# A hybrid attention and delta-rule block on one core: the inverse roots of the delta rule's norms, given out turn by turn

## The chip, the cores and the metric

The kernel runs on one core of one Trainium2 chip. The metric is the device time of one execution in microseconds; the median of three runs of the kernel before is 1054.85 us (1052.07 to 1058.07). TensorE (PE in the profile) does the matrix products and transposes, VectorE (DVE), ScalarE (ACT) and GpSimd (POOL) the rest, and SyncE (SP) issues most transfers. Each engine works through its own queue in order.

## The reference

One layer of a streaming encoder on 512 frames of width 1024, with 16 meta tokens ahead. After a layer norm, one projection `h @ w_in` feeds two mixers. One is attention with 8 heads of 64 and a forget gate ("fox" in the names of the kernel). The other is a gated delta rule ("gdn") with 8 heads of 128: queries, keys and values go through a causal convolution of four taps and a silu, then

```python
q_c = _l2norm(q_c); k_c = _l2norm(k_c)          # x * rsqrt(sum(x*x) + 1e-6)
# in chunks of 64: k, v, beta, decay -> triangular solve, state update, o
o = o * rsqrt(mean(square(o)) + 1e-6) * gdn_norm_w
o = o * silu(z_b)
mixed = sigmoid(gate_a) * (y_a @ w_out_a) + sigmoid(gate_b) * (y_b @ w_out_b)
h = _layer_norm(ALPHA * h + mixed @ w_o)
h = _layer_norm(ALPHA * h + (silu(h @ w_gate) * (h @ w_up)) @ w_down)
```

The two `rsqrt` that the change concerns are those of the norms of q and k, and that of the output `o`, one of each for every delta-rule head.

## The kernel before

The core runs through three stretches: the input (norm and transposes) and the mixers until some 570 us of the span, then the output projections, then the feed-forward network. All products are made in parts of a split of the fp32 operands (`x_hi`, `x_lo` by `wh_`, `wl_`).

**The mixer** is a loop over units (L1240), each a projection of 128 columns of `w_in`: `q`, `k`, `v` and `z` of the eight delta-rule heads, and `qa`, `ka`, `va` of the four pairs of attention heads. TensorE's products of a unit are the main stream. After every few of them `tick` (L627) lets side tasks put in their own instructions. A side task is a Python generator that yields `at(time, banks, uses)`: the planner's estimate of when it may go on, the accumulator banks it needs, and the engines that must not be too far behind. The planner keeps an estimated clock for each engine (`est_t`), works out with costs of its own when an operand is ready (`rdy`), and from that the order of the instructions on TensorE, VectorE, ScalarE and GpSimd is fixed when the kernel is built. What stands between two yields goes out in one piece. `SELF` is the planner's delay between two dependent operations of one engine (0.13 us), `MARGIN` a reserve of 1 us on an estimated arrival. At run time each engine takes its instructions in that order and waits where an operand is not there.

**The side tasks of a delta-rule head.** `conv_finish` (L648) takes a unit's accumulator `ps_q`, `ps_k` or `ps_v` and adds the taps: the first on ScalarE, three on VectorE (tiles `c_q`, `c_k`, `c_v`); after the third the accumulator is free. A unit cannot begin before the one two earlier is free. `gdn_prepare` (L713) sums the squares of q and k (`ss`), scales k into `kn`, takes the nine inverse roots for each row (`rsqrt`, L217; tiles `rst_kq` and `rsy_kq`), makes from them `rq` and `bk`, and then the products `psgm` and `psg` of k with k and with q, which VectorE scales into `nm` and `ea`. `rsqrt` is an initial guess from the bits (two operations) and three Newton turns of three operations, eleven in all, each dependent on the one before.

**The side tasks of a group of two heads.** There are four groups, 0 to 3. `gdn_invert` (L797) runs 31 steps of two dependent VectorE operations (`tmp`, `t`) on the 32x32 blocks of both heads, with a yield after every operation. The result goes out to memory (`td`) and comes back in another layout (`tm`, `pm`, `pmm`); then TensorE joins the blocks (`w_g`, `l_g`). `gdn_chunk` runs the state through four chunks. `gdn_finish` (L935) takes the root of the output's mean square (`ov`, then `rst_o` and `rsy_o` of four values a row), GpSimd scales `o` by it (L948), TensorE transposes it (`oT`), and VectorE multiplies it into `y_b`.

**Attention.** The task behind a `qa` unit copies its accumulator into `q_stack` on VectorE and ScalarE, which frees it.

**GpSimd's queue** also issues the transfers `wl_*` (the low parts of the weights, added in flight), and masks (`ea`). SyncE's queue issues weight loads and the round trip of the inversion.

Of the kernel before, what the change touches and what calls it, by code (L numbers as in the profile page):

```python
# [8 lines left out]
F32 = mybir.dt.float32  # L9
F32R = mybir.dt.float32r  # L10
BF16 = mybir.dt.bfloat16
I32 = mybir.dt.int32
AF = mybir.ActivationFunctionType
ALU = mybir.AluOpType
# [4 lines left out]
P = 128  # L19
# [21 lines left out]
LOOK, MARGIN, CAP = 0.4, 1.0, 0.6  # L41
BUSY = {'dve': 3.0, 'act': 1.0}
LAT, SELF, DMA_LAT, DMA_FINE = 0.15, 0.13, 2.3, 2.5
# [34 lines left out]
def hybrid_block(ctx, tc, x, meta_tokens, ln_in_g, ln_in_b, w_in, b_f, conv_w, a_log, dt_bias,  # L78
# [10 lines left out]
    small = ctx.enter_context(tc.tile_pool(name="small", bufs=4))  # L89
# [6 lines left out]
    est_t = dict.fromkeys(("pe", "act", "dve", "pool", "sp"), 0.0)  # L96
# [3 lines left out]
    def tname(v):  # L100
        t = getattr(v, "tensor", None)
        return getattr(t, "name", None)

    def after(when, name, eng, same=0.0):
        t, by = when.get(name, (0.0, eng))
        return t + (same if by == eng else LAT)
# [20 lines left out]
    def xbank(name):  # L127
        i = min((i for i in order if i not in held),
                key=lambda i: max(after(wrote, banks.get(i, ""), ""), after(read, banks.get(i, ""), "")) if held_on[0] else 0.0)
        order.remove(i)  # L130
        order.append(i)
        t = recycle(("x", i), 1, ps_x.tile([P, 512], F32, tag=f"x{i}", name=name, bufs=1))
        banks[i] = tname(t)
        if held_on[0]:
            held.add(i)
        return t
# [3 lines left out]
    def done(*tiles):  # L140
        for t in tiles:
            held.difference_update([i for i in range(4) if banks.get(i) == tname(t)])
# [56 lines left out]
    class Ordered:  # L199
# [3 lines left out]
        def __getattr__(self, op):  # L203
            fn = getattr(self.eng, op)

            def call(*a, **k):
                ins = fn(*a, **k)  # L207
                account(self.name, op, a, k)
                if pinned[0] and self.name in PINS and op != "dma_start":
# [4 lines left out]
    pe, act, dve, pool, sp = (Ordered(e, n) for e, n in ((nc.tensor, "pe"), (nc.scalar, "act"), (nc.vector, "dve"),  # L214
                                                         (nc.gpsimd, "pool"), (nc.sync, "sp")))

    def rsqrt(v, n, name, eng=nc.vector):  # L217
        rows = v.shape[0]
        y = small.tile([P, n], F32, tag=f"rs_y{n}", name=f"rsy_{name}")[:rows]
        t = small.tile([P, n], F32, tag=f"rs_t{n}", name=f"rst_{name}")[:rows]  # L220
        dve.tensor_scalar(t.bitcast(I32), v.bitcast(I32), 1, None, ALU.logical_shift_right)
        dve.tensor_scalar(y.bitcast(I32), t.bitcast(I32), -1, 0x5F3759DF, ALU.mult, ALU.add)
        for _ in range(3):
            eng.tensor_mul(t, y, y)
            if eng is pool:
                eng.tensor_mul(t, t, v)
                eng.tensor_scalar(t, t, -0.5, 1.5, ALU.mult, ALU.add)
                eng.tensor_mul(y, y, t)
            else:
                eng.scalar_tensor_tensor(t, t, -0.5, v, ALU.mult, ALU.mult)  # L230
                eng.scalar_tensor_tensor(y, t, 1.5, y, ALU.add, ALU.mult)
        return y

    class Pinned:
        def __init__(self, eng):
# [225 lines left out]
    def scaled0(i, eng):  # L461
        gi, k = divmod(i, KT)
        c0 = PAD if gi == 0 else PAD + META + 2 * P
        n = META + 2 * P if gi == 0 else 2 * P
        hf = p1.tile([P, META + 2 * P], F32, tag="hf", name=f"hf{gi}_{k}", bufs=HF)[:, :n]
        g, b = prm[:, k:k + 1], prm[:, 8 + k:9 + k]
        if eng is act_:
            eng.activation(hf, hfs[i][:, :n], AF.Identity, bias=b, scale=g)
        else:
            eng.tensor_scalar(hf, hfs[i][:, :n], g, b, ALU.mult, ALU.add)  # L470
        hfs[i] = hf, x_hi[:, k, c0:c0 + n], x_lo[:, k, c0:c0 + n]
# [4 lines left out]
    def low0(i, eng):  # L476
        eng.tensor_sub(hfs[i][2], hfs[i][0], hfs[i][1].bitcast(F32))
# [13 lines left out]
    for step, *a in START:  # L491
        dict(E=lambda: act_.activation(warm, warm, AF.Exp), F=gate_load, b=lambda t, j: sum_half(t, j), m=meta_sums, v=meta_var, i=invert, y=polish, n=norm, M=meta_norm, p=prm_first,
             W=lambda n: split_high(n), w=lambda n, e: split_low(n, engines[e]), T=transposed,
             f=lambda i, e: scaled0(i, engines[e]), h=high0, l=lambda i, e: low0(i, engines[e]),
# [99 lines left out]
    RS = pool if ON_POOL else dve  # L594
    side = []

    def rdy(*aps):
        return max(after(wrote, tname(v), "") for v in aps) + MARGIN

    def at(t, banks=0, uses=""):  # L600
        return t, banks, uses
# [111 lines left out]
    def gdn_prepare(hd, st):  # L713
        h, hh = hd["h"], hd["hh"]
# [4 lines left out]
        ss = small.tile([P, 9], F32, tag="ss", name=f"ss{h}")  # L719
# [24 lines left out]
        dve.tensor_tensor(kn[:, 0:4, :], by_chunk(psk), kd[:, 0:4].unsqueeze(2).broadcast_to([P, 4, P]), ALU.mult)  # L744
        dve.tensor_scalar(kn[:META, 4, :], psm[:META, :P], kd[:META, 4:5], None, ALU.mult)
        done(psk, psm)
        rs = rsqrt(ss, 9, f"kq{h}", RS)
        rq = hd["rq"] = small.tile([P, 4], F32, tag="rq", name=f"rq{h}", bufs=5)
        RS.tensor_scalar(rq, rs[:, 4:8], P ** -0.5, None, ALU.mult)
        RS.tensor_mul(rs, rs, ss)  # L750
# [184 lines left out]
    def gdn_finish(hd, st):  # L935
        h, o, rq = hd["h"], hd["o"], hd["rq"]
        ov = small.tile([P, 4], F32, tag="ov", name=f"ov{h}")
        yield at(rdy(o), 0, "act")
        scr = gp.tile([P, P], F32, tag="scr", name=f"oscr{h}", bufs=1)
        for c in range(NT):  # L940
            act.activation(scr, o[:, c, :], AF.Square, accum_out=ov[:, c:c + 1])
        yield at(rdy(ov))
        RS.tensor_mul(ov, ov, rq)
        RS.tensor_mul(ov, ov, rq)
        RS.tensor_scalar(ov, ov, 1.0 / P, NORM_EPS, ALU.mult, ALU.add)
        ro = rsqrt(ov, 4, f"o{h}", RS)
        RS.tensor_mul(ro, ro, rq)
        pool.tensor_tensor(o, o, ro.unsqueeze(2).broadcast_to([P, NT, P]), ALU.mult)  # L948
        yield at(rdy(o), 1)
        pt = xbank(f"oT{h}")  # L950
        for c in range(NT):
            pe.transpose(pt[:, c * P:(c + 1) * P], o[:, c, :], ident)
        dve.scalar_tensor_tensor(y_b[h], pt, gdn_w, y_b[h], ALU.mult, ALU.mult)
        done(pt)
        if h < 4:
            sp.dma_start(y_d[h // 2, :, h % 2], y_b[h])
        st["finished"] += 1
# [205 lines left out]
    for g in range(4):  # L1163
        for step in ORDERS[min(g, len(ORDERS) - 1)].split():
            h = 2 * g + int(step[1])
            if step[0] in "qkv":
                w = "qkv".index(step[0])
                unit(f"{step[0]}{h}", (C_QB, C_KB, C_VB)[w] + h * P, conv_halves,
                     lambda ps, h=h, w=w: conv_finish(h, w, ps))
# [70 lines left out]
    for u, d in enumerate(units):  # L1240
# [24 lines left out]
        for n, (o, c) in enumerate(passes):  # L1265
# [6 lines left out]
            if d["name"] == "f":  # L1272
                o, low = [v[:6 * HEADS] for v in o], None
# [414 lines left out]
    for j, u in enumerate(units_f):  # L1688
# [19 lines left out]
        p1, t, v = (fin.tile([P, 256], F32, tag="u2", name=f"u{i}_{j}", bufs=5) for i in range(3))  # L1708
# [77 lines left out]
    ov = out.rearrange("(t p) d -> p t d", p=P)  # L1786
# [88 lines left out]
```

## Time and profile before

| | |
|---|---|
| median of three runs | 1054.85 us |
| the profiled execution | 1061.21 us, span 1059.5 us |
| mean granted clock of TensorE | 0.976 of full speed |
| busy, share of the span | PE 94%, DVE 65%, ACT 48%, POOL 31% |
| chain that ended last, by engine | PE 55%, DVE 21%, issue 7%, DMA 6%, ACT 5%, POOL 2% |

The profile is of one execution, which took 0.6% more than the median. Busy time of an engine is the time in which it has an instruction in work. The chain goes back from the last instruction to what released each step. "Granted clock" is the share of TensorE's full clock that it was given. An arrow `x<-y` in a wait says who waited for whom; in an operation it is output and input. Names have their buffer numbers left out, so `c_v` is that of any head.

### The profile page before, as it was taken

The numbers are of one execution on the slowest core, as the hardware profiler recorded it, in microseconds if no ns is written. First come the engines' busy times: TensorE is split into PE (matmuls) and PEld (weight loads), VectorE is DVE, ScalarE is ACT, GpSimd is POOL, SyncE is SP. The second block draws the span as 40 slices with busy tenths as digits, with TensorE's granted clock in tenths as the row PEclk, the third lists the DMA queues.
The fourth block names the chain that finished last, engine by engine and source line by source line (L and its number), as shares of the span: only waits on it lengthen the run. The fifth ranks groups of instructions, "written<-read, shape, count | busy, mean of one in ns | idle before, by whom it ended". The sixth has DMA issues, their size and how long they took to land.

```text
span 1059.5 us, 17755 instructions
## 1 busy us (share of the span) xinstructions
PE 996.5 (94%) x6765; PEld 890.1 (84%) x6765; DVE 683.8 (65%) x1487; ACT 513.0 (48%) x1039; POOL 327.2 (31%) x338
## 2 busy tenths in 40 slices
PE   5998999999999999999999999988999999999995
PEld 4887998779888898877887888788999999988885
DVE  7446586367936884582153655787998998962436
ACT  6466566554664567454563224744435344531121
POOL 5223212202230122211026200555555556226005
PEclk9998999998999999999999999998999999999998
DMA  7587645626763485467677335525332442344322
GB/s 220 133 182 165 135 107 127 149 51 158 153 142 83 101 196 126 83 150 164 163 194 180 114 110 175 104 61 137 88 115 81 119 120 80 100 140 125 94 80 79
DMA packets 171585, 134.70 MB, mean 127 GB/s; under 512 B 19820, under 2 KB 151180, under 8 KB 171500
## 3 DMA queue, kind: packets, MB, share of 16 engines
q1 hardware_dynamic: 161788, 98.39, 32.9%
q0 software_dynamic: 9712, 35.18, 17.6%
q8 instruction: 53, 0.87, 0.3%
q14 instruction: 32, 0.26, 0.1%
HBM read 90.90 MB, written 8.57 MB: 94 GB/s over the span
## 4 chain that ended last, share of the span: by engine, by line
PE 55%; DVE 21%; issue 7%; DMA 6%; ACT 5%; POOL 2%; SPq 0%; DVEq 0%; POOLq 0%; ACTq 0%
PE d L1366 3%; PE d L1364 3%; PE d L1365 3%; PE ps_v L207 3%; PE px L1454 3%; PE ptm L207 3%; PE o L240 3%; PE ps_q L207 2%; PE ps_ga L207 2%; PE ps_z L207 2%; PE ps_gb L207 2%; PE ps_va L207 2%; PE ps_k L207 2%; PE po L1321 2%; PE po L1319 2%
## 5 line engine op out<-in xcount | busy, mean ns | idle before, releaser
L285 DVE TENSOR_TENSOR wl_d<-wr_d,wh_d 128x1024 fp32r<-128x1024 f32 x18 | 22.7, 1263 | 51.4 <-ACT wh_d L283 51.4
L283 ACT CAST wh_d<-wr_d 128x1024 fp32r<-128x1024 f32 x18 | 18.9, 1050 | 65.9 <-PE d L1366 44.0
L1488 POOL TENSOR_TENSOR wr_a<-wr_a,sums 128x512 f32<-128x512 f32 x22 | 29.1, 1323 | 57.1 <-DVE wl_a L1428 56.9
L207 DVE TENSOR_TENSOR tmp<-n,t 34x31 f32<-34x31 f32 (+15 forms) x124 | 42.8, 345 | 2.0
L207 DVE TENSOR_TENSOR t<-t,tmp 34x31 f32<-34x31 f32 (+15 forms) x124 | 42.4, 342 | 1.9
L1365 PE MATMUL d<-wl_d,f_h 128*128 128x512 f32 (+1 forms) x104 | 39.7, 381 | 0.0
L1364 PE MATMUL d<-wh_d,f_h 128*128 128x512 f32 (+1 forms) x104 | 39.6, 381 | 0.0
L1454 PE MATMUL pa<-v_h,wh_a 128*128 128x256 f32 x160 | 39.3, 279 | 0.0
L1454 PE MATMUL pa<-v_h,wl_a 128*128 128x256 f32 x160 | 39.1, 280 | 0.0
L283 ACT CAST wh_wo<-wr_wo 128x512 fp32r<-128x512 f32 (+1 forms) x16 | 13.3, 836 | 40.5 <-PE po L1320 13.8
L285 DVE TENSOR_TENSOR wl_wo<-wr_wo,wh_wo 128x512 fp32r<-128x512 f32 (+1 forms) x16 | 22.5, 1418 | 15.2 <-ACT wh_wo L283 15.2
L1428 DVE TENSOR_TENSOR wlo_b<-wr_b,whi_b 128x1024 fp32r<-128x1024 f32 x11 | 21.7, 1976 | 16.4 <-ACT whi_b L1427 16.4
L1454 PE MATMUL px<-v_h,rb 128*128 128x256 f32 x176 | 26.5, 295 | 4.5 <-DMA rb<-sums 4.5
L1454 PEld LDWEIGHTS pa<-v_h,wh_a 128*128 128x128 f32 x160 | 30.2, 189 | 0.0
L1673 ACT ACTIVATE res<-res 128x512 f32<-128x512 f32 x11 | 7.0, 633 | 47.7 <-DVE res L1738 47.7
L1454 PEld LDWEIGHTS pa<-v_h,wl_a 128*128 128x128 f32 x160 | 30.0, 187 | 0.0
L207 ACT COPY o<-ks 128x128 f32<-128x128 f32 x32 | 8.5, 266 | 44.2 <-DVE r L207 44.2
L207 DVE SCALAR_TENSOR_TENSOR r<-ks,nbeg,bv 128x128 f32<-128x128 f32 x32 | 11.2, 351 | 28.6 <-PE ks L207 23.5
L1454 PEld LDWEIGHTS px<-v_h,rb 128*128 128x128 f32 x176 | 24.2, 203 | 4.7 <-DMA rb<-sums 4.7
L1427 ACT CAST whi_b<-spare_raw 128x1024 fp32r<-128x1024 f32 x10 | 10.5, 1052 | 35.4 <-PE pd L1454 35.4
L207 PE MATMUL ps_z<-x_hi,wh_z 128*128 128x512 f32 x64 | 27.4, 427 | 0.0
L207 PE MATMUL ps_z<-x_lo,wh_z 128*128 128x512 f32 x64 | 27.2, 425 | 0.0
(800 smaller groups left out, 3681.6 us busy)
## 6 DMA issues: line engine op xcount, KB each, us to landing
wr_d<-in_w_down_dram SPq DMA_DIRECT2D x18, 512.0 KB, 3.7
spare_raw<-in_w_gate_dram SPq DMA_DIRECT2D x11, 512.0 KB
wr_b<-in_w_up_dram SPq DMA_DIRECT2D x11, 512.0 KB, 3.8
wr_a<-in_w_gate_dram SPq DMA_DIRECT2D x11, 512.0 KB
wr_a<-in_w_up_dram SPq DMA_DIRECT2D x11, 512.0 KB, 5.4
wr_k<-in_w_in_dram SPq DMA_DIRECT2D x8, 512.0 KB, 5.6
wr_q<-in_w_in_dram SPq DMA_DIRECT2D x8, 512.0 KB, 4.3
wr_z<-in_w_in_dram SPq DMA_DIRECT2D x8, 512.0 KB, 5.2
```

Of the source, the lines that this page charges most:

```text
L207: ins = fn(*a, **k)
L240: return lambda *a, **k: tc.keep_in_program_order(fn(*a, **k))
L283: nc.scalar.copy(hi[:, :k * n], raw[:, :k * n])
L285: eng.tensor_sub(lo[:, :k * n], raw[:, :k * n], hi[:, :k * n].bitcast(F32))
L1319: nc.tensor.matmul(g[:, j, :], wh[:, i, :], hi[i], start=i == 0, stop=False)
L1321: nc.tensor.matmul(g[:, j, :], wl[:, i, :], hi[i], start=False, stop=i == k - 1)
L1364: nc.tensor.matmul(acc, ah, wh[:, cols], start=kk == 0, stop=False)
L1365: nc.tensor.matmul(acc, ah, wl[:, cols], start=False, stop=False)
L1366: nc.tensor.matmul(acc, al, wh[:, cols], start=False, stop=kk == ktiles - 1)
L1428: order(eng.tensor_sub(lo, src, hi.bitcast(F32)))
L1454: order(nc.tensor.matmul(dst, a[:, k, :], v[i][:, k, :], start=n == 0, stop=n == 11))
L1488: pin(nc.gpsimd.tensor_sub(v1[:, 1], v1[:, 1], sums[:, 0]))
```

## The change

A new function `rsqrt_turns` gives the same eleven operations as a generator, with a yield ahead of each of the three turns. `gdn_prepare` yields once before the root of q and k and at each turn, `gdn_finish` at each turn, both with the condition that the inversion's steps have: VectorE's estimated time plus `SELF`. Before GpSimd's scaling of `o` there is now a yield until the estimated end of the root. The instructions are the same, in number and in kind; their order follows from the planner.

```diff
--- before.py
+++ after.py
@@ -230,6 +230,21 @@
                 eng.scalar_tensor_tensor(t, t, -0.5, v, ALU.mult, ALU.mult)
                 eng.scalar_tensor_tensor(y, t, 1.5, y, ALU.add, ALU.mult)
         return y
+
+    def rsqrt_turns(v, n, name):
+        y = small.tile([P, n], F32, tag=f"rs_y{n}", name=f"rsy_{name}")
+        t = small.tile([P, n], F32, tag=f"rs_t{n}", name=f"rst_{name}")
+
+        def turns():
+            dve.tensor_scalar(t.bitcast(I32), v.bitcast(I32), 1, None, ALU.logical_shift_right)
+            dve.tensor_scalar(y.bitcast(I32), t.bitcast(I32), -1, 0x5F3759DF, ALU.mult, ALU.add)
+            for _ in range(3):
+                yield
+                dve.tensor_mul(t, y, y)
+                dve.scalar_tensor_tensor(t, t, -0.5, v, ALU.mult, ALU.mult)
+                dve.scalar_tensor_tensor(y, t, 1.5, y, ALU.add, ALU.mult)
+
+        return y, turns()
 
     class Pinned:
         def __init__(self, eng):
@@ -744,7 +759,10 @@
         dve.tensor_tensor(kn[:, 0:4, :], by_chunk(psk), kd[:, 0:4].unsqueeze(2).broadcast_to([P, 4, P]), ALU.mult)
         dve.tensor_scalar(kn[:META, 4, :], psm[:META, :P], kd[:META, 4:5], None, ALU.mult)
         done(psk, psm)
-        rs = rsqrt(ss, 9, f"kq{h}", RS)
+        yield at(est_t["dve"] + SELF, 0, "dve")
+        rs, turns = rsqrt_turns(ss, 9, f"kq{h}")
+        for _ in turns:
+            yield at(est_t["dve"] + SELF, 0, "dve")
         rq = hd["rq"] = small.tile([P, 4], F32, tag="rq", name=f"rq{h}", bufs=5)
         RS.tensor_scalar(rq, rs[:, 4:8], P ** -0.5, None, ALU.mult)
         RS.tensor_mul(rs, rs, ss)
@@ -943,8 +961,11 @@
         RS.tensor_mul(ov, ov, rq)
         RS.tensor_mul(ov, ov, rq)
         RS.tensor_scalar(ov, ov, 1.0 / P, NORM_EPS, ALU.mult, ALU.add)
-        ro = rsqrt(ov, 4, f"o{h}", RS)
+        ro, turns = rsqrt_turns(ov, 4, f"o{h}")
+        for _ in turns:
+            yield at(est_t["dve"] + SELF, 0, "dve")
         RS.tensor_mul(ro, ro, rq)
+        yield at(rdy(ro) - MARGIN)
         pool.tensor_tensor(o, o, ro.unsqueeze(2).broadcast_to([P, NT, P]), ALU.mult)
         yield at(rdy(o), 1)
         pt = xbank(f"oT{h}")
```

On VectorE, at head 1 of group 0, the end of the chain of `gdn_prepare` and what follows it before the change (128x9 are the root's operations, 128x528 a tap of the convolution):

```order
L207 TENSOR_TENSOR rst_kq_1098<-rsy_kq_1097 128x9
L207 SCALAR_TENSOR_TENSOR rst_kq_1098<-rst_kq_1098,ss_1035 128x9
L207 SCALAR_TENSOR_TENSOR rsy_kq_1097<-rst_kq_1098,rsy_kq_1097 128x9
L207 TENSOR_SCALAR rq_1110<-rsy_kq_1097 128x4
L207 TENSOR_TENSOR rsy_kq_1097<-rsy_kq_1097,ss_1035 128x9
L207 TENSOR_TENSOR bk_1113<-rsy_kq_1097,beta 128x4
L207 TENSOR_TENSOR bk_1113<-rsy_kq_1097,beta 128x1
L207 SCALAR_TENSOR_TENSOR c_v_1070<-ps_v_923,prm,c_v_1070 128x528 x3
L207 SCALAR_TENSOR_TENSOR nm_1148<-psgm_1146,r_1090,em_1014 16x16
```

and the same chain in the order of the change, from its last operation ahead of the root on:

```order
L207 TENSOR_SCALAR kn_1038<-psm_1041,kd_1092 16x128
L207 SCALAR_TENSOR_TENSOR c_v_1070<-ps_v_923,prm,c_v_1070 128x528
L207 TENSOR_SCALAR rst_kq_1099<-ss_1035 128x9
L207 TENSOR_SCALAR rsy_kq_1098<-rst_kq_1099 128x9
L207 SCALAR_TENSOR_TENSOR c_v_1070<-ps_v_923,prm,c_v_1070 128x528
L207 TENSOR_TENSOR rst_kq_1099<-rsy_kq_1098 128x9
L207 SCALAR_TENSOR_TENSOR rst_kq_1099<-rst_kq_1099,ss_1035 128x9
L207 SCALAR_TENSOR_TENSOR rsy_kq_1098<-rst_kq_1099,rsy_kq_1098 128x9
L207 SCALAR_TENSOR_TENSOR c_v_1070<-ps_v_923,prm,c_v_1070 128x528
L207 TENSOR_TENSOR rst_kq_1099<-rsy_kq_1098 128x9
L207 SCALAR_TENSOR_TENSOR rst_kq_1099<-rst_kq_1099,ss_1035 128x9
L207 SCALAR_TENSOR_TENSOR rsy_kq_1098<-rst_kq_1099,rsy_kq_1098 128x9
```

The three taps of `c_v`, which stood behind the chain, now stand ahead of the root, behind its two bit operations, and behind the first turn; `nm` still follows `bk`.

On TensorE, around the end of head 5's `ps_v` (the second head of group 2, whose q and k have been projected; `k4T` is the key of head 4), before the change:

```order
L207 MATMUL ps_v_3342<-x_hi,wl_v_3247 128x268 x16
L207 MATMUL ps_qa_3442<-x_hi,wh_qa_3350 128x512
L207 MATMUL psgm_3455<-k4T 16x16
L207 MATMUL psg_0_3460<-k4T 128x128
L207 MATMUL psg_0_3460<-qf_3154,k4T 128x128
```

and, further on in the order before, where the first join of group 1 (`w_1`) stands, at the start of `ps_va`:

```order
L207 MATMUL ps_ka_3586<-x_hi,wl_ka_3450 128x264 x2
L207 MATMUL ps_va_3689<-x_hi,wh_va_3591 128x264 x2
L207 MATMUL w_1_3704<-tm_2475,ea_1678 32x32 x8
L207 MATMUL w_1_3704<-tm_2475,ea_2131 32x32 x8
L207 MATMUL ps_va_3689<-x_lo,wh_va_3591 128x264 x2
```

The same stretch in the order of the change, from the last products of head 5's `ps_v` on:

```order
L207 MATMUL ps_v_3382<-x_lo,wh_v_3291 128x268 x2
L207 MATMUL psv_3470<-ident,v4T 128x128 x4
L207 MATMUL psw_3471<-ident,v4T 16x128
L207 MATMUL ps_v_3382<-x_hi,wl_v_3292 128x268 x2
L207 MATMUL w_1_3484<-tm_2427,ea_1679 32x32 x8
L207 MATMUL w_1_3484<-tm_2427,ea_2120 32x32 x8
L207 MATMUL ps_v_3382<-x_hi,wl_v_3292 128x268 x14
L207 MATMUL ps_qa_3520<-x_hi,wh_qa_3389 128x512
L207 MATMUL l_1_3531<-ws_3485,pm_2424 32x32
```

The transposes `psv` and `psw` of head 4 and both products `w_1` now stand inside `ps_v`, the products `l_1` behind the first product of `ps_qa`; before, `psgm` and `psg` of head 4 stood in `ps_qa` and `w_1` two units later, in `ps_va`.

## Rows read from the trace of the kernel before

**Rows 1.** The page, part 1: busy us (share of the span) xinstructions of each engine.

```profile
PE 996.5 (94%) x6765; PEld 890.1 (84%) x6765; DVE 683.8 (65%) x1487; ACT 513.0 (48%) x1039; POOL 327.2 (31%) x338
```

**Rows 2.** Windows, core 0: us; busy us of each engine; granted clock, DMA share, GB/s.

```profile
50.00:600.00 550.00, 521.31 (x3691) 460.76 (x3692) 325.03 (x941) 305.02 (x731) 126.77 (x167) 0.97 0.62 140
```

**Rows 3.** TensorE's waits, 60 to 560 us: waiting tile, releaser, us in total, times, longest.

```profile
PE ps_ka L207 <- DVE nm L207: 3.5, 1, 3.5
PE ps_qa L207 <- DVE c_q L207: 2.6, 1, 2.6
PE oT L207 <- POOL o L207: 2.5, 2, 2.4
...
PE l L207 <- DMA pm<-td: 1.8, 1, 1.8
PE ps_va L207 <- DVE q_stack L207: 1.7, 1, 1.7
...
PE ps_qa L207 <- DMA wl_qa<-wr_qa: 1.4, 1, 1.4
```

**Rows 4.** Timeline of VectorE, 94 to 99.8 us: start, us, engine, line, operation.

```profile
94.33 0.15 DVE L207 TENSOR_SCALAR rst_kq<-ss 128x9 int32<-128x9 int32 x1
...
96.36 0.17 DVE L207 SCALAR_TENSOR_TENSOR rsy_kq<-rst_kq,rsy_kq 128x9 f32<-128x9 f32 x1
...
97.12 2.37 DVE L207 SCALAR_TENSOR_TENSOR c_v<-ps_v,prm,c_v 128x528 f32<-128x528 f32 x3
99.41 0.21 DVE L207 SCALAR_TENSOR_TENSOR nm<-psgm,r,em 16x16 f32<-16x16 f32 x1
```

**Rows 5.** Windows after three of TensorE's waits, same columns as rows 2.

```profile
99.70:107.00 7.30, 7.30 (x40) 7.30 (x41) 5.66 (x7) 2.27 (x3) 5.18 (x9) 0.63 0.77 181
283.00:287.00 4.00, 4.00 (x21) 3.43 (x22) 3.68 (x9) 0.47 (x1) 0.98 (x2) 0.62 0.54 117
366.30:372.00 5.70, 5.70 (x46) 5.50 (x47) 5.37 (x10) 3.49 (x5) 2.62 (x3) 1.00 0.50 95
```

**Rows 6.** Timeline of VectorE, 256 to 283 us: tap, inversion and chain of heads 4, 5.

```profile
267.29 0.38 DVE L207 TENSOR_TENSOR tmp<-n,t 34x231 f32<-34x231 f32 x1
...
268.44 0.75 DVE L207 SCALAR_TENSOR_TENSOR c_k<-ps_k,prm,c_k 128x528 f32<-128x528 f32 x1
...
277.43 0.15 DVE L207 TENSOR_SCALAR rst_kq<-ss 128x9 int32<-128x9 int32 x1
...
280.22 0.76 DVE L207 SCALAR_TENSOR_TENSOR c_q<-ps_q,prm,c_q 128x528 f32<-128x528 f32 x1
...
281.08 1.56 DVE L207 SCALAR_TENSOR_TENSOR c_q<-ps_q,prm,c_q 128x528 f32<-128x528 f32 x2
```

**Rows 7.** Timeline of TensorE, 262 to 284 us.

```profile
274.03 0.41 PE L207 MATMUL ps_v<-x_hi,wh_v 128*128 128x268 f32 x2
...
282.79 0.76 PE L207 MATMUL ps_qa<-x_hi,wh_qa 128*128 128x512 f32 x1 [2.60 <-DVE c_q L207]
```

**Rows 8.** Timeline of SyncE's queue, 286 to 305 us: the round trip of group 1.

```profile
291.78 0.36 SPq L207 DMA_DIRECT2D td<-t  x1
...
300.62 2.70 SPq L207 DMA_DIRECT2D pm<-td  x4
```

**Rows 9.** Timeline of SyncE's queue, 386 to 405 us: the round trip of group 2.

```profile
387.47 0.26 SPq L207 DMA_DIRECT2D td<-t  x1
```

**Rows 10.** Timeline of TensorE, 401 to 410 us: what that trip releases.

```profile
407.23 0.18 PE L207 MATMUL l<-pm,ws 32*32 32x32 f32 x1 [1.83 <-DMA pm<-td]
```

**Rows 11.** Chain of waits, 298 to 304 us: start, us, what.

```profile
300.87 0.68 DVE q_stack L207
```

**Rows 12.** Timeline of VectorE, 364 to 367.5 us.

```profile
365.25 1.17 DVE L207 TENSOR_TENSOR tmp<-n,t 34x231 f32<-34x231 f32 x1
```

**Rows 13.** Timeline of GpSimd, 350 to 373 us.

```profile
365.13 1.03 POOL L207 TENSOR_TENSOR o<-o,rsy_o 128x512 f32<-128x512 f32 x1
```

**Rows 14.** Tile view of the output roots: GpSimd's idle time before scaling, releaser, times.

```profile
  DVE rsy_o L207: 18.4, 5
```

## The prediction

> **What bounds the kernel now.** I read the page's busy times first. TensorE is busy 996.5 of 1059.5 us, VectorE 683.8 [rows 1]: the kernel is bound by TensorE's own work, and the change touches none of it. What it can win is time in which TensorE stands still, and only while the mixer runs. There TensorE is busy 521.31 of 550 us [rows 2], so 28.7 us of idle time is the ceiling, with whatever a lowered clock after a pause adds. Next the list of TensorE's waits [rows 3], which says what a root chain could have to do with: `ps_ka` 3.5 us behind `nm`, `ps_qa` 2.6 behind `c_q`, `oT` 2.5 behind GpSimd's scaling of `o`, `ps_va` 1.7 behind `q_stack`. That is 10.3 us in four places. The rest of that list waits for transfers or for other engines. Then the timelines around these places, and the granted clock after them.
>
> **What one chain costs.** The timeline of VectorE ahead of the longest wait has the eleven root operations of head 1 in a row, first start 94.33, last start 96.36, last length 0.17: 2.20 us, or 0.20 us for each, every one waiting for the one before it. Behind them, and four short operations, stand the three taps of `c_v`, 2.37 us [rows 4]. The taps do not need the roots. The change removes and adds no instruction: 16 chains, each cut at three points, 48 in all; in the order of the change other VectorE work stands at 32 of these, in the other 16 the next turn follows at once. So the sum is one of waits alone, place by place.
>
> **Place A, head 1.** In the new order a tap stands ahead of the root, one after the two bit operations, one after the first turn. From the start of the root to the end of the third tap that is five root operations at 0.20 and 2.37 us of taps: 94.33 + 1.0 + 2.37 = 97.7, where it was 97.12 + 2.37 = 99.49. TensorE's `ps_ka`, which now comes ahead of `psgm` and so no longer behind `nm`, gains 1.8 us. `nm`, the four `ea` and `bk` come later than they would without the taps among them, but their cover is the `ps_ka` products that now run beside them. The clock: in the 7.3 us after this 3.5 us pause the granted clock was 0.63, between the levels 1.2 and 2.4 GHz, a loss of 7.3 x 0.37 = 2.7 us; after the 2.6 us pause before `ps_qa` it was 0.62 over 4.0 us, a loss of 1.5; after the pause of 2.4 before `oT` it was 1.00 [rows 5]. A pause of 1.7 is left at A, and the nearest row is the one at 1.00: I take 2.7 back (bounds 0 and 2.7). A gives 4.5.
>
> **Place C, head 4.** `ps_qa` starts at 282.79 after a wait of 2.60 [rows 7], behind the third `c_q` tap, which ends at 281.08 + 1.56 = 282.64; that stood behind the whole chain of head 4, begun at 277.43 [rows 6]. In the new order the taps are spread among turns, `nm` and two `ea`, so the third tap is hardly earlier. But TensorE has work in front of it: `psgm`, both `psg`, `psv` and the 32 products of `w_1`, all formerly inside or behind `ps_qa`, now stand in `ps_v`. Filler is as good as an earlier tap: the 2.6 us go (bounds 0 and 2.6), and with no pause the 1.5 us of clock. C gives 4.1.
>
> What is late next at C is the round trip of the inversion. VectorE's inversion of group 1 has done 17 of 31 steps, not 12, when the taps of head 4's key come, so it ends before the taps of head 5's key, which began at 268.44 [rows 6]. Its matrices go out to memory and come back before `w_1` and `l_1` can use them, and everything of TensorE is queued behind these two. In group 1 the trip took from 291.78 until the last `pm` load was issued at 300.62 + 2.70 = 303.32, so at least 11.5 us [rows 8]; in group 2 it took from 387.47 [rows 9] to the matmul that waited for it at 407.23, 19.8 us [rows 10]. From 268.4 that lands between 280.0 and 288.2. `l_1` comes at the earliest at 282.79 - 2.60 + 0.76, some 281 with the first `ps_qa` product, and later by the filler. The wait is 0 to 7 us; I take 2.0, nearer to the trip of the same group.
>
> **Place D, head 5.** `q_stack` starts at 300.87 [rows 11], when the chain of head 5 is out of VectorE's way, and `ps_va` waits 1.7 for it. That chain is still in one piece in the new order; it is only that five inversion steps fewer lie ahead of it. Bounds 0 and 1.7; I take 0.8.
>
> **Place E, heads 2 and 3.** In the trace both output chains run whole, and `o` of head 2 is scaled only at 365.13 [rows 13], 2.4 us after `oT` could have begun [rows 3]. GpSimd stands idle 18.4 us in five such waits [rows 14]. The new order puts `oT` of head 2 at the end of `ps_k` and that of head 3 well into `ps_q`, with attention between; on GpSimd the scaling of the one is apart from that of the other. The rest of GpSimd's waits has cover: TensorE had only 2.5 us of waits for scaling in all. I take 2.4 (bounds 0 and 2.4).
>
> **The port.** One price speaks against the change. At 365.25 an inversion product of 34x231 took 1.17 us [rows 12], while GpSimd scaled `o` from 365.13 for 1.03 [rows 13]; the same shape took 0.38 without it [rows 6]. So 0.79 us for each scaling that meets inversion work, at most 8 x 0.79 = 6.3 us of VectorE's time. The interleaving puts inversion steps right beside turns and scalings. Much of VectorE's time is slack, so I take 1.0 (bounds 0 and 6.3).
>
> The Trainium skill, SBUF — State Buffer, section "SBUF: two separate sides", says that VectorE with two SBUF inputs and GpSimd take their shared ports as an exclusive lock, one blocking the other wholly. By that rule the inversion product should have run 1.03 + 0.38 - 0.12 = 1.29 us from its start, against the 1.17 of the trace, and the root turns, which read two SBUF tiles as well, would be blocked too. By the lock the sum would have the whole 6.3 in the place of 1.0, as a rival does below.
>
> **Given back.** The other waits at `ps_qa` and `l` are for transfers (`wl_qa` 1.4, `pm` 1.8 [rows 3]); a transfer doesn't come earlier because TensorE does. Of what is won ahead of them part returns there: 0 to 3.2, I take 2.0.
>
> **The sum.** 4.5 + 4.1 + 0.8 + 2.4 = 11.8, less 2.0 for `l_1`, 1.0 for the port, 2.0 given back: 6.8. The profiled execution took 1061.21 us, so 1054.4; it lay 0.6% above the median of three, 1054.85, and scaled by that ratio the forecast is 1048. About 0.5%, 5 us, is what a measurement can tell from no change here, so 1048 lies only just outside of it.
>
> **The rivals.**
> *The gain is hidden.* A's and C's waits move on to the next buffer, transfer or tap: five of the places are behind units whose taps come one unit later anyway. For it: D, unbroken, shows a chain that is late one unit after C's. Against it: two units after A and C have no wait of note. Then the clock's 4.2 and half of the other 7.6 are lost, and the 3.0 for `l_1` and the port stay: 3.8 - 3.0, a gain near 1, 1054.
>
> *The round trip takes the place of the wait, slower.* `w` and `l` stand in TensorE's order ahead of `ps_qa` by a planner's guess of the trip. If the trip in groups 1 and 2 takes the 19.8 us of group 2, both wait up to 7 us, each pause costs 1.5 to 2.7 of clock, and C's 4.1 is lost: 14 + 4 + 3 - 7.7 = 13 slower, 1068 on the median's scale. With a trip halfway, 15.7, it is 3 for each wait, 5 slower, 1060. I take 1064 between them. It decides from a trip of about 13 us (281 less 268.4). For it: `pm` was waited for already in group 2; weights load at the same time. Against: group 1's own trip may have been just 12.
>
> *The port decides.* All eight scalings meet inversion work on VectorE's late stretches: 5.3 us more than I took, 1053.
>
> *It doesn't do what it says.* Turns run on in a row, at 16 of 48 points in the new order; if only those chains mattered the time stays at 1055. Head 1's order is against it.
>
> **How the numbers follow.** Forecast 0.47, alone between 1042 and 1054; hidden 0.26; round trip 0.18; port 0.06; no change 0.03. Below 1049.6 lie three quarters of the forecast (0.35), a quarter of the hidden and port cases (0.08): faster 0.43. Above 1060.1 lie four fifths of the round trip (0.14), and some 0.06 of the rest: slower 0.20. Between them 0.37. For 8 in 10 the range reaches from the forecast's low end with more clock back, 1040, to the middle of the slower rival's own span, 1063.
>
> **What would show it.** Right: `ps_ka` waits under 2 us at head 1, with the granted clock near 1 after it; no wait at `ps_qa` of head 5; the three `c_v` taps apart on VectorE; `oT` of head 2 without a wait. Wrong: a wait of `w` or `l` for `tm` or `pm` in groups 1 or 2 of over 2 us; inversion products over 1 us at more than four scalings; the waits for weight transfers grown by as much as the others fell. Waits that go while the span stays would say that TensorE's clock or its own work, not VectorE, sets the end.

## The result: slower, and the profile after

The change made the kernel slower: a median of 1065.3 us in four runs (1062.46 to 1069.28) against 1054.03 us, ratio 1.0084 with a 95% interval of 1.0055 to 1.0114. Run again beside two other kernels it was 1065.16 us, 1.0077 (1.0044 to 1.0111). The prediction had 1048 us.

The profiled execution of the change has a span of 1060.7 us, only 1.2 us more than the one of before, whose execution (1061.21 us) lay above the median of 35 later runs of that kernel, 1057.5, while the change's (1062.46 us) was the shortest of its four. Two single executions must not be set against each other by their spans, then; what can be compared is where TensorE stands still. The stretch of [rows 2] in the window view of the change:

```profile
50.00:600.00 550.00, 515.61 (x3681) 455.13 (x3680) 319.31 (x940) 304.37 (x730) 125.78 (x167) 0.98 0.61 140
```

The second number is TensorE's busy time, 515.61 of 550 us: 34.4 us of idle time where [rows 2] had 28.7. A second profiled execution of the change had 33.3. Of that loss of 5.7 us the list of TensorE's waits, the same view as [rows 3], gives the names:

```profile
PE w L207 <- DMA tm<-td: 5.7, 3, 3.6
PE pt L207 <- ACT pr L207: 5.6, 3, 3.0
PE ps_ga L207 <- DMA wl_ga<-wr_ga: 4.1, 2, 2.9
PE ps_qa L207 <- DMA wl_qa<-wr_qa: 2.9, 1, 2.9
...
PE psg L207 <- DVE nm L207: 2.2, 1, 2.2
...
PE oT L207 <- POOL o L207: 1.3, 1, 1.3
PE psv L207 <- DVE v1T L207: 1.2, 1, 1.2
PE ps_ka L207 <- DVE rst_kq L207: 1.2, 1, 1.2
PE l L207 <- DMA pm<-td: 0.8, 2, 0.7
```

Of the four waits that the prediction was about, `ps_ka` fell from 3.5 to 1.2 and `oT` from 2.5 to 1.3; those of `ps_qa` for `c_q` and of `ps_va` for `q_stack` are gone. At the head of the list stands one that was not there: `w`, the join of the inverted blocks, waits 5.7 us for `tm` on its way back from memory, and `l` 0.8 for `pm`. Idle time is not the whole loss. In ten later runs of the change the mean granted clock was 0.976, in 27 runs of the kernel before beside them 0.982.

On VectorE at head 1, where [rows 4] had the taps behind the whole chain, they now come apart, with turns between:

```profile
93.50 0.75 DVE L207 SCALAR_TENSOR_TENSOR c_v<-ps_v,prm,c_v 128x528 f32<-128x528 f32 x1
...
94.44 0.76 DVE L207 SCALAR_TENSOR_TENSOR c_v<-ps_v,prm,c_v 128x528 f32<-128x528 f32 x1
95.12 0.16 DVE L207 TENSOR_TENSOR rst_kq<-rsy_kq 128x9 f32<-128x9 f32 x1
...
95.60 0.76 DVE L207 SCALAR_TENSOR_TENSOR c_v<-ps_v,prm,c_v 128x528 f32<-128x528 f32 x1
```

and on TensorE, the waits in that place:

```profile
91.87 3.41 PE L207 MATMUL ps_qa<-x_hi,wl_qa 128*128 128x512 f32 x8 [2.93 <-DMA wl_qa<-wr_qa]
96.51 0.48 PE L207 MATMUL ps_ka<-x_hi,wh_ka 128*128 128x264 f32 x2 [1.23 <-DVE rst_kq L207]
...
105.71 0.66 PE L207 MATMUL psv<-ident,v1T 128*128 128x128 f32 x4 [1.24 <-DVE v1T L207]
```

The third tap ends at 95.60 + 0.76 = 96.36 and `ps_ka` begins at 96.51. But ahead of it the wait for the weights `wl_qa` is 2.9, where [rows 3] had 1.4, and behind it `psv` waits 1.2 for `v1T`, which had no wait of note.

The round trips of the change, on SyncE's queue, are to be set beside [rows 8, 9]. Group 0:

```profile
171.71 0.25 SPq L207 DMA_DIRECT2D td<-t  x1
172.87 0.23 SPq L207 DMA_DIRECT2D td<-n  x1
178.31 0.40 SPq L207 DMA_DIRECT2D wr_z<-in_w_in_dram  x1
179.73 3.19 SPq L207 DMA_DIRECT2D tm<-td  x3
183.01 3.08 SPq L207 DMA_DIRECT2D pm<-td  x4
```

and the joins on TensorE, in groups 0, 1 and 2:

```profile
187.39 0.24 PE L207 MATMUL w<-tm,ea 32*32 32x32 f32 x2 [3.56 <-DMA tm<-td]
```

```profile
291.62 0.18 PE L207 MATMUL l<-ws,pm 32*32 32x32 f32 x1 [0.65 <-DMA pm<-td]
```

```profile
395.36 1.00 PE L207 MATMUL w<-tm,ea 32*32 32x32 f32 x32 [1.89 <-DMA tm<-td]
```

In group 0 the inverse left at 171.71 and `w` could begin at 187.39, 15.7 us later. A weight load (`wr_z`) is between the trip's parts in the queue, and the loads of `tm` and `pm` take some 3 us to issue. TensorE had come to `w` 3.56 us before. In the second profiled execution of the change `w` waits 3.8 us in group 0 as well; the 1.7 that it waits in group 2 are put down to `ea` of VectorE there, so the 1.89 may not be the trip's alone. The window view shows what else that costs, granted clock third from the end:

```profile
187.40:200.00 12.60, 10.17 (x137) 9.23 (x138) 2.41 (x10) 6.85 (x13) 2.19 (x4) 0.79 0.58 136
200.00:215.00 15.00, 15.00 (x102) 13.56 (x102) 2.56 (x7) 5.39 (x14) 4.18 (x8) 0.83 0.37 82
```

Neither of these stretches has the whole clock (0.79 and 0.83). By the prediction's own way of counting, that is an estimated 12.6 x 0.21 + 15.0 x 0.17 = 5.2 us more than the pause itself. In [rows 5] two of three pauses were followed by a lowered clock as well.

### The profile page after: what moved, and what is told of

It is laid out like the page before. It is cut to its first block, busy times and chain, and to the rows that moved or that the text cites. A ratio compares the mean times of both kernels' runs of the same rounds, so it can differ in the third digit from the quotient of the medians.

```text
span 1060.7 us, 17749 instructions
## 1 busy us (share of the span) xinstructions
PE 993.4 (94%) x6765; PEld 887.0 (84%) x6765; DVE 681.9 (64%) x1487; ACT 512.5 (48%) x1039; POOL 327.0 (31%) x338
## 4 chain that ended last, share of the span: by engine, by line
PE 49%; DVE 15%; DMA 7%; issue 5%; ACT 3%; POOL 2%; SPq 0%; DVEq 0%; POOLq 0%; ACTq 0%
PE o L255 3%; PE ps_ga L207 3%; PE d L1387 3%; PE d L1385 3%; PE d L1386 3%; PE ps_gb L207 3%; PE px L1475 3%; PE ps_z L207 2%; PE po L1342 2%; PE po L1340 2%; PE po L1341 2%; DMA wl_ga<-wr_ga 2%; PE ptm L207 2%; PE ps_v L207 2%; DVE wl_a L1449 2%
## 5 line engine op out<-in xcount | busy, mean ns | idle before, releaser
L300 DVE TENSOR_TENSOR wl_d<-wr_d,wh_d 128x1024 fp32r<-128x1024 f32 x18 | 26.3, 1461 | 47.9 <-ACT wh_d L298 47.9
L300 DVE TENSOR_TENSOR wl_wo<-wr_wo,wh_wo 128x512 fp32r<-128x512 f32 (+1 forms) x16 | 21.7, 1364 | 15.3 <-ACT wh_wo L298 15.3
L207 PE MATMUL ps_v<-x_hi,wh_v 128*128 128x268 f32 x128 | 28.1, 302 | 0.0
L207 PE MATMUL ps_v<-x_lo,wh_v 128*128 128x268 f32 x128 | 27.6, 298 | 0.0
```

The source lines that it names most:

```text
L300: eng.tensor_sub(lo[:, :k * n], raw[:, :k * n], hi[:, :k * n].bitcast(F32))
```

## Experiments

Each ratio is that of a kernel to the one before on the same chip, with its 95% interval.

### Is it the turns, or the scaling?

**e1_kq_only** keeps `rsqrt` in `gdn_finish`, **e2_o_only** keeps it in `gdn_prepare`, **e3_pool_only** keeps both whole and only adds the yield before GpSimd's scaling, and **e4_head1_only** gives out the turns at head 1 alone:

```diff
 # e3_pool_only
+        yield at(rdy(ro) - MARGIN)
         pool.tensor_tensor(o, o, ro..., ALU.mult)
 # e4_head1_only
+        if h == 1:
+            yield at(est_t["dve"] + SELF, 0, "dve")
```

> Only the root of the norms of q and k is given out in turns; the output's root and GpSimd's scaling are as before. Theory R (the round trip: the inversions' joins w and l come earlier in TensorE's order and wait for tm and pm): the turns of q and k move the inversion, so this part alone has the waits of w and l above 4 us in all and is 0.5 to 1% slower than before, about 1063. Theory O (the output's chains and the later scaling are the fault): this is as before or up to 3 us faster, 1051 to 1055. Theory P (any change of the planner's input gives out another order, with a time of its own): somewhere in 1050 to 1066, its waits at other places than those of the whole change.

> Only the output's root is given out in turns and GpSimd's scaling waits for it; the root of q and k is as before. Theory R: about as before, 1052 to 1056, with w and l waiting no more than the 2.4 us of before. Theory O: 1060 to 1066, with scaling or attention waits (pt behind pr) over 4 us. Theory P: 1050 to 1066, with waits at places of its own.

> Only the yield before GpSimd's scaling is added; both roots are in one piece as before. Theory R: as before, 1053 to 1055. Theory O: part of the loss, 1057 to 1060. Theory P: although nothing on the path is added or split, the time moves by more than 3 us either way, since the order on TensorE changes in group 1 and after.

> The turns of q and k are given out at head 1 alone, where the longest wait of before is; all other roots in one piece. Theory R: the wait at ps_ka falls from 3.5 to under 2 us and nothing else is worse, so 2 to 4 us faster, 1050 to 1052. Theory P: the wait at ps_ka falls just so, but the order behind it changes as much as with the whole change, and the time is anywhere in 1050 to 1066.

| kernel | median, us | ratio |
|---|---|---|
| e1_kq_only | 1071.4 | 1.0126 (1.0088 to 1.0164) |
| e2_o_only | 1066.61 | 1.0082 (1.0053 to 1.0110) |
| e3_pool_only | 1070.36 | 1.0122 (1.0094 to 1.0150) |
| e4_head1_only | 1067.13 | 1.0090 (1.0059 to 1.0121) |

Every part alone costs as much as the whole or more (the intervals overlap). So no part is the culprit, and the losses don't add. Their waits are in part at different places. First e3, then e4:

```profile
PE oT L207 <- POOL o L207: 10.0, 4, 4.6
...
PE w L207 <- DMA tm<-td: 1.8, 1, 1.8
```

```profile
PE oT L207 <- POOL o L207: 7.4, 4, 3.3
PE ps_qa L207 <- DMA wl_qa<-wr_qa: 6.3, 2, 3.5
...
PE ps_ka L207 <- DVE rst_kq L207: 2.1, 1, 2.1
```

In e3 `oT` waits 10.0 us for the scaling that its yield puts off; in e2, which has the same yield, such waits come to 0.3. In e4 `ps_ka` of head 1 fell from 3.5 to 2.1 us, the joins do not wait at all, and yet it is as slow as the change, with waits for scaling and for weights. Theories R and O, as the one cause for all these kernels, fall: R expected e2, e3 and e4 no slower than before, O expected e1 no slower. What R said of e1 came true in kind, for `w` waits 5.0 us for `tm` there too. Theory P is the one left, but it is vague, and three of its ranges were missed: e1 with 1071.4, e2 with 1066.61 and e4 with 1067.13 all lie above 1066.

### Is another order slower in itself?

**n1_look** and **n3_look** are the kernel before with one number of the planner changed:

```diff
-LOOK, MARGIN, CAP = 0.4, 1.0, 0.6
+LOOK, MARGIN, CAP = 0.42, 1.0, 0.6     # n1_look; 0.38 in n3_look
```

> The kernel before, with one number of the planner altered that stands for nothing on the chip (how far it looks ahead, 0.42 for 0.40 us). The roots are in one piece as before; the order of instructions on TensorE, VectorE and ScalarE differs in about one row in four. Theory P: the time moves by more than 3 us, most likely slower, 1058 to 1068, with new waits at places of its own. A theory by which only the turns or the later scaling cost time: 1053 to 1057.

> The kernel before with the planner's look ahead at 0.38 for 0.40 us, the other side of the run at 0.42; the roots are whole, the order differs in some 40% of TensorE's rows and more of VectorE's. Theory P: slower than before by 3 to 12 us, 1060 to 1069, with other waits than at 0.42 and than with the change. A theory by which the order before is no better than others: 1053 to 1060, either side of before.

n1 took 1063.28 us, 1.0048 (1.0030 to 1.0066), and n3 1059.93 us, 1.0029 (1.0011 to 1.0047). Both are slower, neither has any turn; n3 is a hair below the 1060 that theory P expected. In n1 the waits are at the taps:

```profile
PE ps_v L207 <- DVE c_k L207: 7.7, 2, 5.4
PE ps_va L207 <- DMA wl_va<-wr_va: 3.7, 1, 3.7
...
PE ps_ka L207 <- DVE c_v L207: 3.1, 1, 3.1
```

All six kernels with an order of their own, and the change, are slower than the kernel before, by 0.3 to 1.3%. So the order of before is a good one among its neighbours, and each of these seven other orders started some 3 to 13 us behind. It is no law: k1 below, an eighth order, is not measurably slower.

### Does the splitting cost?

**h1_after_gathered** has the change's order on the other engines, but holds back the instructions of each root until its last turn, while the planner counts them where it did:

```diff
+                if kept[0] is not None and self.name == "dve":
+                    account(self.name, op, a, k)
+                    kept[0].append(lambda: tc.keep_in_program_order(fn(*a, **k)))
+                    return None
```

> The order of the changed kernel on TensorE, ScalarE, GpSimd and SyncE, but on VectorE every root's eleven operations stand in one piece where its last turn stood, so no turn is between other work. Theory P (the loss comes with the new order of all engines): as the changed kernel within 4 us, 1061 to 1069. A theory by which splitting the chains costs by itself (the port between VectorE and GpSimd, or a stop at every boundary): back to before, 1053 to 1057.

It took 1065.58 us, 1.0075 (1.0047 to 1.0103), as the change itself. `pt` and `w` are in front again; `psw` waits 4.2 us where the change had 0.5, in an execution that was the longest of seven:

```profile
PE pt L213 <- ACT pr L213: 5.0, 3, 2.5
PE psw L213 <- DVE nm L213: 4.2, 2, 3.2
PE w L213 <- DMA tm<-td: 3.8, 1, 3.8
```

So splitting the roots costs nothing, and brings nothing, beyond the 3 us that either interval leaves open.

h1 does not price the port, for three of its scalings are long too (1.36 to 1.38). The traces do say that the change made little difference to it. Three of the change's 248 inversion operations took over 0.8 us, as in the kernel before; one of the three stood beside a scaling (1.29 us at 360.72). Three of its eight scalings took over 1.3 us (1.36 to 1.39), before two (1.35 and 1.37). And in the chain of the output's root three operations, 0.16 us elsewhere, took 1.05, 1.73 and 1.77 beside a scaling; in the kernel before it was one of 1.73 and two pairs of 1.19 and 1.22. The clearest:

```profile
456.16 1.04 POOL L207 TENSOR_TENSOR o<-o,rsy_o 128x512 f32<-128x512 f32 x1
456.17 1.05 DVE L207 TENSOR_SCALAR rst_o<-ov 128x4 int32<-128x4 int32 x1
```

VectorE's operation begins just behind GpSimd's and ends with it, 0.9 us late. That one of the two can block the other is what the Trainium skill says (SBUF — State Buffer, section "SBUF: two separate sides"), and here the trace agrees with it. The other two of VectorE's began 0.3 us ahead of the scaling, and why they and some scalings took longer is not shown.

### Were the sums at A, C and D right?

**f2_heads_moved** uses the same holding back on the kernel before. The planner gives out the order of before, and on VectorE alone the roots of three heads move behind what waits:

```diff
 VectorE, head 1 (kernel before -> f2)
+SCALAR_TENSOR_TENSOR c_v<-ps_v,prm,c_v 128x528 x3
 TENSOR_SCALAR rst_kq<-ss 128x9
...
-SCALAR_TENSOR_TENSOR c_v<-ps_v,prm,c_v 128x528 x3
 # so for head 4 (c_q, one step t) and head 5 (q_stack x2)
```

> The planner runs as in the kernel before and gives the same order on TensorE, ScalarE, GpSimd and SyncE; on VectorE alone the root of q and k of heads 1, 4 and 5, with rq and bk, is moved in one piece behind what waits next: the three taps of c_v, the three taps of c_q, the two q_stack. Theory L (the local arithmetic of places A, C and D holds, and the loss of the change is that of the new order): the waits at ps_ka 3.5, ps_qa 2.6 and ps_va 1.7 fall to under 1 us in all, and the time falls by 5 to 8 us, 1047 to 1050. Theory H (such waits only move on to the next buffer or transfer): other waits grow by as much, 1053 to 1056.

It took 1051.36 us, 0.9946 (0.9923 to 0.9969): 5.7 us faster than before, and the fastest kernel of this study that leaves nothing out. The gain lies in theory L's 5 to 8 us; the time lies above its 1047 to 1050, since the kernel before took 1057.69 beside it. TensorE's idle time is 23.9 us and the granted clock 0.99:

```profile
50.00:600.00 550.00, 526.08 (x3739) 462.84 (x3738) 331.50 (x951) 308.87 (x736) 126.67 (x167) 0.99 0.61 142
```

```profile
95.63 0.48 PE L217 MATMUL ps_ka<-x_hi,wh_ka 128*128 128x264 f32 x2 [0.58 <-DVE rst_kq L215]
```

```profile
PE oT L217 <- POOL o L217: 2.9, 2, 2.8
...
PE psv L217 <- DVE v1T L217: 1.9, 1, 1.9
PE l L217 <- DMA pm<-td: 1.5, 3, 0.8
...
PE w L217 <- DMA tm<-td: 0.9, 1, 0.9
```

`ps_ka` waits 0.6, `ps_qa` for `c_q` and `ps_va` for `q_stack` not at all: 7.8 us of waits went to 0.6. New are `psv` behind `v1T` (1.9) and `w` (0.9). Theory L holds: where the plan is kept, waits that go give time back, 5.7 us for 7.2. The prediction's own terms (1.8 at A, 0.8 at D, the clock) are not tested by it one by one, for here whole roots move, and none is split.

**f3_more_moved** moves head 6's root too, behind the last inversion step of group 2:

```diff
+            if g == 2 and j == BLK - 2:
+                give(6)
```

> The kernel before with the roots of heads 1, 4 and 5 moved behind what waits next, as before, and that of head 6 moved behind the last step of group 2's inversion, so that its round trip begins some 2.6 us earlier; the rest of the order is kept. Theory L: the wait of l for pm in group 2 goes as well, 1 us or less more than with three heads, 1049 to 1052. Theory H: the trip's loads meet the weight loads, nothing gained, 1051 to 1053.

It took 1054.37 us, 0.9976 (0.9959 to 0.9992): less good than f2, though the two intervals just overlap, and above what either theory expected. The queue of SyncE came out otherwise as well (`tm` ahead of a weight load), and `w` and `l` wait more, not less, 3.9 us together:

```profile
PE w L217 <- DMA tm<-td: 2.3, 2, 1.4
...
PE l L217 <- DMA pm<-td: 1.6, 3, 1.2
```

The trip of group 2 began at 375.63, where f2 had 378.52, and its last `pm` load was issued by 396.26, where f2 had 394.02. A trip that begins earlier was not a shorter one; why is not settled.

### What is the round trip worth?

**g1_after_short_trip** is the change, **g0_before_short_trip** the kernel before, both planned as they are, but `tm`, `pm` and `pmm` are loaded from the blocks that went into the inversion:

```diff
-            sp.dma_start(tm[32 * b:32 * b + 32, :, c:c + 32], tv[0, b])
+            load(tm[32 * b:32 * b + 32, :, c:c + 32], tv[0, b], b, 32, 8, 4)
 # load: account(...) as for tv, then a transfer of the same bytes from nd
```

> The changed kernel, planned the same, but tm, pm and pmm are loaded from the blocks that went into the inversion, not from its result, so the loads wait for nothing (this leaves the inverse out of what follows; bytes and descriptors are the same). Theory R (the round trip is the main cause): w and l wait under 1 us in all instead of 6.5, and 6 to 10 us go, 1055 to 1059. Theory P (many places share the loss): 3 to 6 us go at most, 1059 to 1062, and waits for wl and for pr stay.

> The control to the changed kernel with the short trip: the kernel before, planned the same, with tm, pm and pmm loaded from the blocks that went into the inversion (the inverse is left out of what follows). Theory R: the trip was a cause only in the changed kernel; here the wait of l for pm (1.8 us) goes and the time falls by 1 to 4 us, 1053 to 1056. Theory D (the short trip, or what it loads, makes any kernel faster, by the clock or by freeing the queue): 8 us or more go, 1046 to 1049.

g1 took 1052.53 us, 0.9956 (0.9934 to 0.9978), g0 1052.92 us, 0.9962 (0.9946 to 0.9978). On the chip of each, the change gets 1065.16 - 1052.53 = 12.6 us back, more than either theory expected, and the kernel before 1057.5 - 1052.9 = 4.6, about what theory R expected. The difference, 8.0 us, is about all that the change lost (0.0077 x 1056.76 = 8.1). With the short trip the two orders are equal, within some 3 us. In the window view of g1:

```profile
50.00:600.00 550.00, 523.03 (x3743) 460.63 (x3742) 327.59 (x952) 308.65 (x736) 125.76 (x167) 0.99 0.62 142
```

TensorE is busy 523.03 us where the change had 515.61: 7.4 us of idle time went, about the 6.5 of `w` and `l`. The rest of the 12.6 is clock, as far as the rows show: the stretches that had 0.79 and 0.83 in the change have all of it here,

```profile
187.40:200.00 12.60, 10.43 (x137) 9.04 (x136) 5.06 (x15) 7.64 (x17) 6.73 (x12) 1.00 0.75 164
200.00:215.00 15.00, 14.51 (x101) 12.62 (x99) 5.84 (x22) 5.78 (x18) 1.46 (x4) 1.00 0.54 112
```

and over all runs the mean granted clock is 0.985, where it was 0.976. Other data in the joins is no part of the difference between g1 and g0, since both have the same. The edit does one thing more than its name says: loads that wait for nothing go out early, in group 2 of g1 at 308.85, while the inverse leaves at 372.04. So it takes away the wait and the loads' place in SyncE's queue together. That the freed queue brought weights sooner is not seen: TensorE's waits for `wl_*` are 10.4 us in g1 and 10.6 in the change.

**g2_short_group0** has the short trip in group 0 only, **g3_short_groups123** in the other three; **after_again** is the change beside them (`if not (g == 0)`, or `if not (g > 0)`, ahead of the whole trip in `load`).

> The changed kernel with the short trip in group 0 alone (its inverse is left out of what follows; groups 1 to 3 make the whole trip). If the loss sits at the longest wait of the trace, w of group 0 behind tm, 3.6 us and the lowered clock after it: 5 to 8 us of the 12.8 that all four short trips gave go here, 1057 to 1060. If it sits in groups 1 and 2, as the prediction's rival had it: 0 to 3 us, 1062 to 1066.

> The changed kernel with the short trip in groups 1 to 3 and the whole one in group 0 (the inverses of groups 1 to 3 are left out of what follows). If the loss sits in group 0: 4 to 7 us go, 1058 to 1061, with w of group 0 still waiting 3.6 us. If it sits in groups 1 and 2: 9 us or more, 1053 to 1056.

> The changed kernel itself, once more beside the two before on the same chip. By all theories 0.6 to 1.1% slower than before, 1062 to 1069.

g2 took 1057.57 us, 1.0008 (0.9983 to 1.0032), g3 1055.67 us, 0.9995 (0.9973 to 1.0018), the change 1065.16. Either gives back most of the loss, 7.6 and 9.5 us. Together that is more than the 12.6 of both, but by less than the intervals leave open (some 2.5 us either way for each ratio). Each time fits the theory that puts the loss there, so the two theories were no alternatives: the loss sits in no one group, and about half of it in each part.

**k1_after_late_join** leaves the trip whole and lets the planner give out the joins later:

```diff
-        yield at(rdy(tm, pm, pmm), 1)
+        yield at(rdy(tm, pm, pmm) + 4.0, 1)
```

> The changed kernel with one number more in the planner: the joins w, l of the inversion are given out 4 us later than the estimated arrival of tm and pm. The round trip and its result are whole. Theory R: w and l wait under 2 us in all, and the time falls to 1054 to 1059. Theory P (any new order has waits of its own): the waits of w and l go as well, but others take their place, 1060 to 1066.

It took 1059.85 us, 1.0020 (0.9994 to 1.0047), with runs from 1052.43 to 1067.67: between what theory R (to 1059) and theory P (from 1060) expected. No wait of `w` or `l` for the trip is left in its list, which is from the shortest of the twelve runs; the first are:

```profile
PE pt L207 <- ACT pr L207: 4.5, 3, 2.6
PE ps_ga L207 <- DMA wl_ga<-wr_ga: 3.6, 1, 3.6
PE oT L207 <- POOL o L207: 3.1, 4, 1.3
```

By the ratios, 1.0020 for 1.0077, some three quarters of the loss come back by one number, with an interval that allows from two fifths to all; other waits take part of the place.

## Why the prediction was wrong, step by step

**The waits that go: right.** The prediction took 1.8 at A, 2.6 at C, 0.8 at D and 2.4 at E, 7.6 us without the clock. The four waits of [rows 3] fell from 10.3 to 2.5, by 7.8. A measured 2.3 (3.54 to 1.23), C and D went whole. E's wait went whole too, and another `oT`, at 251.34, now waits 1.3. The signs of being right that the prediction named came true, and its three of being wrong did not: `w` and `l` wait 0.8 us in group 1 and 1.9 in group 2, under the 2 us that it named. The longest wait of the trip, in group 0, none of its signs covered. Its last sign, waits that go while the span stays, came, but not for the reason that it gave: TensorE's idle time grew.

**The clock at A: it came back, and went elsewhere.** 2.7 us were to come back after `ps_ka`. They did, but part of it was lost ahead of it:

```profile
91.87:96.50 4.63, 3.40 (x8) 2.18 (x9) 4.32 (x16) 4.57 (x10) 0.86 (x1) 0.63 0.50 127
96.50:104.00 7.50, 7.49 (x62) 7.32 (x63) 2.88 (x13) 4.62 (x6) 2.53 (x5) 1.00 0.77 165
```

The granted clock is 1.00 behind `ps_ka`, and 0.63 ahead of it, behind the wait for `wl_qa`: 4.63 x 0.37 = 1.7 us. With 1.5 more of wait for `wl_qa` and 1.2 at `psv`, A's 2.3 + 2.7 shrinks to an estimated 0.6. The wait for `wl_qa` is not the change's doing alone: it is 1.3 in f2 and 3.0 in f3, with one order on TensorE.

**What takes its place: the step that failed.** The sum subtracted 2.0 for `l_1`, 1.0 for the port and 2.0 given back, 5.0 in all. Measured: idle time rose by 5.7 while 7.8 went, so 13.5 us of other waits came. Of these 4.7 are the round trip (6.5 against the 1.8 of [rows 3, 10]), 4.5 attention (`pt` behind `pr`, 5.6 where it had been 1.1), 2.2 `psg` behind `nm`, and 3.3 weights (10.6 for `wl_*`, where it was 7.3); some smaller waits went. The sum also counted 4.2 us of clock as won, and the runs' mean clock fell from 0.982 to 0.976. The term for the trip was formed for group 1 alone, where it came out at 0.8. That is near the 2.0 by luck: the inverse left at 274.58 and not by 268.4, and `l_1` came at 291, not 281. The term was not formed at all for group 0, where the wait is 3.8, and group 2 with 1.9. On the prediction's own measure, from `td` until the last `pm` load is issued, the trips of groups 0 to 2 took 14.4, 15.4 and 15.3 us. In the kernel before they had taken 16.1, 11.5 and 15.5, so the sum leaned on the shortest of them. The trip to `w` took 15.7 and 14.0 us there (from 171.71 to 187.39, and from 381.32 to 395.36), and at most 13.3 in group 1 (274.58 to 287.83, without a wait of `w`). The experiments settle that this term, with the loads' place in the queue, decides between the two orders: g1 against g0. It does not decide between others: e4 has no wait at the joins and is as slow.

**The rival was right in kind; its price was luck.** "The round trip takes the place of the wait" had 1064, with a point of decision at a trip of 13 us. But its price was for waits of 3 to 7 us at both `w` and `l` in groups 1 and 2, with C's gain lost and 3.0 for `l_1` and the port. Measured were 2.7 in these groups, 3.8 in group 0, which it left out, and C's wait gone. 0.18 was too little: the trace of before already had a trip of 19.8 us and a wait for `pm`, and the new order put the joins nearer to the end of the inversion in three groups (0, 2 and 3).

**The port: wrong as a danger.** 1.0 us was subtracted for it. The trace of the change has one inversion product over 1 us beside a scaling, as before, and no more slow small operations; no run prices the port by itself. "It doesn't do what it says" was wrong as well: the turns are apart.

**A case that was missing.** "Any new order starts behind" stood in none of the rivals. Two orders that differ from the one before by a number without meaning are 0.3 and 0.5% slower. Neither trace nor diff of the change shows it; that the planner goes by estimates of 0.4 and 1.0 us, the size of the waits at stake, might have been a hint.

What stays open: why `pt` waits more for `pr` in the new order (5.6 us; it is still 5.2 in g1, which is fast all the same), and why f3 is slower than f2.

## What to carry to other kernels

Where a planner fixes the order of everything, a local edit is not local: sum the waits that it removes, and then look in the new order at each place where one engine stands close behind a transfer, in every group. To find out what a local edit is worth, keep the plan and move the instructions by themselves; that gave 5.7 us here where the re-planned change lost 8 to 9. And compare with an order that was changed for no reason, before a difference below 1% is put down to a reason.

## What the runs showed of the hardware

A pause of TensorE can cost more than its length. In the change `w` of group 0 waits 3.8 us, and in the 27.6 us behind it the granted clock was 0.79 and 0.83, an estimated 5.2 us more; with the short trip there is no such pause, and the same stretches have 1.00. Not every pause is followed by that: after the third of [rows 5] the clock was 1.00. The profiled executions of the change and of g1 show it over the whole span, TensorE's line of the page first for the change:

```profile
PE 993.4 (94%) x6765; PEld 887.0 (84%) x6765; DVE 681.9 (64%) x1487; ACT 512.5 (48%) x1039; POOL 327.0 (31%) x338
```

```profile
PE 984.8 (94%) x6765; PEld 879.1 (84%) x6765; DVE 678.3 (65%) x1487; ACT 512.4 (49%) x1039; POOL 327.3 (31%) x338
```

Of the 14.4 us between the spans (1060.7 and 1046.3) only 5.8 are idle time; 8.6 are the same 6765 products done in less time, at a mean granted clock of 0.990 for 0.980.

The same kernel's runs spread by up to 15 us (k1, 1052.43 to 1067.67). In g1 the spread goes with the clock: the longest run (1059.2) had 0.979, the shortest (1048.04) 0.99. In h1 it does not: 1059.84 at 0.979 and 1070.87 at 0.98. What else spreads the runs is open.
